# A four-layer transformer pass on one core: TensorE's order written out in the source, attention in bundles, and a wider up-projection

## The chip, the core and the metric

The kernel runs on one NeuronCore of a Trainium2 chip, in one launch. The metric is device time in microseconds (us) of that core; a profile of one execution lies beside the timed runs. TensorE does the matmuls, with its weight loads shown apart (PEld). VectorE (DVE) and ScalarE (ACT) do the elementwise work, GpSimd (POOL) a few powers and some DMA issues, SyncE (SP) issues most DMAs.

## The reference, cut to what matters

Two blocks of two layers each act on x of 256 tokens by 1024 features, in float32. Every layer is attention, a residual, and an MLP with another residual.

```python
# block 1
x = x + concat(diff_attention(q, k, v), memory_attention(qm, mem)) @ a_w_out      # layer a
x = x + relu(rms(x) @ a_w_up) ** 2 @ a_w_down                                     # 1024 -> 4096 -> 1024
x = x + concat(moba_attention(q, k, v), memory_attention(qm, mem)) @ b_w_out      # layer b
x = x + relu(rms(x) @ b_w_up) ** 2 @ b_w_down
x = rms(x) * final_norm
# block 2
h = h + rms(stick_breaking(q, k, v) @ sb_w_o) * g                                 # 16 heads of 64
h = h + rms(conv_ffn(rms(h)))                                                     # 1024 -> 2 x 2816 -> 1024, gated
h = h + rms(forgetting(q, k, v, fcum) @ fox_w_o) * g
h = h + rms(conv_ffn(rms(h)))
```

conv_ffn is `gelu(conv3(gate)) * conv3(up)` followed by the down-projection. Diff attention is softmax minus lambda times a second softmax, with a norm for each head; with 256 tokens the moba layer is plain causal attention with rope.

## The kernel before

**Numbers in halves.** Weights and activations are float32. Each is split into a high half, rounded to float32r (whi, yTh, L169 or L179 on ScalarE), and the rest (wlo, yTl, L170 or L180 on VectorE). A product is three matmuls, high x high, high x low and low x high (mm3, L206 to L210). The split weights live in eight buffers of 128 x 1024 for each half (W_BUFS, tags whi and wlo), the raw weights in three (RAW_BUFS).

**Projections.** mm_rows (L278) makes a tile of 128 tokens by up to 512 columns: for each of eight k two matmuls with the token tile's high half as weights (L282, L283), then eight with its low half (L285). columns_T (L300) makes 128 columns of y @ w transposed, with all 256 tokens as the moving columns: eight times mm3 in 256 columns.

**MLP.** up_pair (L498) makes two chunks of 128 features in one bank with columns_T; the first group goes by up_tokens (L505), a row tile at a time, and is transposed afterwards. The result goes through relu and a square (mlp, L554) or through the convolution, gelu and product (conv_ffn, L569), is split (u_split, L490) and put to Down (L523), which adds the down-projection up in four banks. Down.put issues the matmuls of the item before; the last three items are done a row tile at a time, with finish(t) after each.

**Attention.** quad (L427) does four heads for a query tile: scores (L344, matmuls on L349), a softmax (soft, L392) or the stick-breaking weights (stick, L410), transposes of the weights (blocks_T, L383, L387), attention times v (L436; L900 in the forgetting layer) and out_T (L403). The differential layer has its own diff (L688), with its heads' norm on "on" (L712) and a transpose. The layers (layer_a L663 on, layer_b, layer_sb, layer_fox) call projections and quads in the order of the source.

**What sets the order.** The order on every engine, TensorE's too, is set by a scheduler from the dependencies, a cost model and the order of the source as priority: a later projection can go ahead of a score that isn't ready, and a group of attention matmuls is cut up and strewn among a projection's. issue_after (L198) holds a few splits back by hand. The eight PSUM banks: two "acc", two "sc", two "ht", one "pt", one "po".

## Time and profile before

| | |
|---|---|
| median of 3 runs | 1265.97 us (1265.57 to 1266.2) |
| span of the profiled execution | 1265.0 us |
| TensorE busy | 1245.0 us (98%), 7791 matmuls |
| weight loads | 1083.7 us (86%) |
| VectorE busy | 873.0 us (69%) |
| ScalarE busy | 744.8 us (59%) |
| DMA | 211.77 MB, mean 167 GB/s |

A busy time is the sum of what one engine had in work. Matmuls are pipelined and their ends are modelled: the spacing of their starts tells what one costs in a stream, not its duration. The stages in order of time: memory keys and values and the start of layer a up to about 52 us, layer a's attention to 150, its MLP to 335, layer b's attention to 450, its MLP to 635, stick breaking to 760, the first gated FFN to 950, forgetting attention to 1075, and the second gated FFN.

### The profile page before, as it was taken

To read this page: it belongs to the slowest core of one execution; us is meant where nothing else is said; L and a number is where in the kernel's file an instruction comes from. 1 tells how busy PE (TensorE), PEld (TensorE's weight loads), DVE (VectorE), ACT (ScalarE), POOL (GpSimd) and SP (SyncE) were. 2 spreads that over 40 slices of the span, in tenths; PEclk is the share of its full clock that TensorE was granted. 3 is DMA by queue.
4 is the path that set the end of the run, shared out by engine and by line. 5 is a ranking of instruction groups with operands and counts; after the bars stand their busy time and mean duration, and the time that the engine had idled before them with its cause. 6 is when DMAs were issued, how large, how long until landed. Compare 5 with 4: busy or idle time off the path is not lost.

```text
span 1265.0 us, 20179 instructions
## 1 busy us (share of the span) xinstructions
PE 1245.0 (98%) x7791; PEld 1083.7 (86%) x7791; DVE 873.0 (69%) x1687; ACT 744.8 (59%) x1386; POOL 43.0 (3%) x73
## 2 busy tenths in 40 slices
PE   8999999999999999999999999999999999999997
PEld 6776789999876789999889778999989987999996
DVE  5778755565887665556567888667678876877675
ACT  7656654444766655445556778555567755855552
POOL 1201100000000000000000000000001000000000
PEclk9999999999999999999999999999999999999999
DMA  9643356464454165646373426555537443655550
GB/s 318 215 167 107 113 174 223 153 214 166 155 178 132 40 210 186 215 152 211 132 240 134 134 79 199 194 169 179 198 96 254 139 149 102 214 191 185 170 173 34
DMA packets 129552, 211.77 MB, mean 167 GB/s; under 512 B 5368, under 2 KB 86624, under 8 KB 129456
## 3 DMA queue, kind: packets, MB, share of 16 engines
q1 hardware_dynamic: 127616, 207.25, 49.0%
q0 software_dynamic: 1696, 3.17, 0.8%
q8 instruction: 61, 1.00, 0.3%
q14 instruction: 35, 0.29, 0.1%
q10 hardware_dynamic: 144, 0.07, 0.0%
HBM read 209.36 MB, written 1.10 MB: 166 GB/s over the span
## 4 chain that ended last, share of the span: by engine, by line
PE 92%; ACT 3%; DVE 2%; DMA 1%; issue 1%; POOL 1%; SPq 0%; POOLq 0%; DVEq 0%; ACTq 0%
PE acc L208 12%; PE acc L209 12%; PE acc L210 12%; PE sc L210 10%; PE sc L208 10%; PE sc L209 10%; PE acc L282 5%; PE acc L283 5%; PE acc L285 5%; PE sc L349 4%; PE tp L387 2%; PE tp L436 2%; PE tp L251 1%; ACT junk L231 1%; DVE wlo L170 1%
## 5 line engine op out<-in xcount | busy, mean ns | idle before, releaser
L170 DVE TENSOR_TENSOR wlo<-raw,whi 128x1024 fp32r<-128x1024 f32 x336 | 403.3, 1221 | 167.3 <-ACT whi L169 163.5
L169 ACT ACTIVATE whi<-raw 128x1024 fp32r<-128x1024 f32 x336 | 343.8, 1055 | 169.8 <-PE acc L210 75.3
L210 PE MATMUL sc<-yTh,wlo 128*128 128x256 f32 x1088 | 308.0, 283 | 0.0
L209 PE MATMUL sc<-yTl,whi 128*128 128x256 f32 x1088 | 308.0, 283 | 0.0
L208 PE MATMUL sc<-yTh,whi 128*128 128x256 f32 x1088 | 307.8, 283 | 0.0
L208 PEld LDWEIGHTS sc<-yTh,whi 128*128 128x128 f32 x1088 | 208.6, 192 | 2.3 <-issue 0.5
L209 PEld LDWEIGHTS sc<-yTl,whi 128*128 128x128 f32 x1088 | 208.6, 192 | 1.7
L210 PEld LDWEIGHTS sc<-yTh,wlo 128*128 128x128 f32 x1088 | 208.6, 192 | 0.1
L208 PE MATMUL acc<-whi,u 128*128 128x512 f32 x432 | 169.2, 392 | 0.0
L209 PE MATMUL acc<-wlo,u 128*128 128x512 f32 x432 | 168.8, 391 | 0.0
L210 PE MATMUL acc<-whi,u 128*128 128x512 f32 x432 | 167.0, 390 | 0.0
L282 PE MATMUL acc<-whi,yTh 128*128 128x512 f32 (+3 forms) x336 | 132.3, 397 | 0.4
L283 PE MATMUL acc<-wlo,yTh 128*128 128x512 f32 (+3 forms) x336 | 130.4, 391 | 0.0
L587 DVE SCALAR_TENSOR_TENSOR cv<-sc,conv,cv 128x255 f32<-128x255 f32 (+1 forms) x160 | 76.2, 479 | 36.7 <-ACT cv L585 35.1
L210 PEld LDWEIGHTS acc<-whi,u 128*128 128x128 f32 x432 | 81.1, 188 | 17.4 <-DVE u L495 0.4
L208 PEld LDWEIGHTS acc<-whi,u 128*128 128x128 f32 x432 | 81.3, 188 | 16.4 <-ACT u L494 0.9
L209 PEld LDWEIGHTS acc<-wlo,u 128*128 128x128 f32 x432 | 81.3, 188 | 14.9
L285 PE MATMUL acc<-whi,yTl 128*128 128x512 f32 (+3 forms) x336 | 85.0, 387 | 0.0
L179 ACT ACTIVATE whi<-raw,g_late 128x256 fp32r<-128x256 f32 (+4 forms) x160 | 71.5, 520 | 18.3 <-PE acc L209 11.1
L180 DVE SCALAR_TENSOR_TENSOR wlo<-raw,g_late,whi 128x256 fp32r<-128x256 f32 (+4 forms) x160 | 72.5, 507 | 11.8 <-ACT whi L179 11.7
L282 PEld LDWEIGHTS acc<-whi,yTh 128*128 128x128 f32 x336 | 63.9, 190 | 12.9 <-ACT yTh L261 2.1
L208 PE MATMUL acc<-yTh,whi 128*128 128x256 f32 x256 | 74.3, 290 | 0.0
(193 smaller groups left out, 1751.5 us busy)
## 6 DMA issues: line engine op xcount, KB each, us to landing
raw<-in_w_up SPq DMA_DIRECT2D x88, 512.0 KB, 4.7
raw<-in_w_down SPq DMA_DIRECT2D x22, 1024.0 KB, 5.4
raw<-in_a_w_up SPq DMA_DIRECT2D x16, 1024.0 KB, 5.5
raw<-in_a_w_down SPq DMA_DIRECT2D x16, 1024.0 KB, 4.9
raw<-in_b_w_up SPq DMA_DIRECT2D x16, 1024.0 KB, 5.4
raw<-in_b_w_down SPq DMA_DIRECT2D x16, 1024.0 KB, 4.8
raw<-in_a_w_in SPq DMA_DIRECT2D x16, 512.0 KB, 5.8
raw<-in_sb_w_qkv SPq DMA_DIRECT2D x16, 512.0 KB, 4.5
```

What stands on the lines that cost most here:

```text
L169: act(hv, rv[:, k0:k1], AF.Copy)
L170: V.tensor_tensor(lv, rv[:, k0:k1], hv.bitcast(F32), op=ALU.subtract)
L179: act(hv[:, k - k0, o:e], rv[:, k, o:e], AF.Copy, scale=gk)
L180: V.scalar_tensor_tensor(lv[:, k - k0, o:e], rv[:, k, o:e], gk, hv[:, k - k0, o:e].bitcast(F32), op0=ALU.mult, op1=ALU.subtract)
L208: mm(acc, lhsT=a[0], rhs=b[0], start=start, stop=False)
L209: mm(acc, lhsT=a[0], rhs=b[1], start=False, stop=False)
L210: mm(acc, lhsT=a[1], rhs=b[0], start=False, stop=stop)
L282: mm(acc, lhsT=h, rhs=ws[k][0], start=k == 0, stop=False)
L283: mm(acc, lhsT=h, rhs=ws[k][1], start=False, stop=False)
L285: mm(acc, lhsT=tslice(yT, k, t)[1], rhs=ws[k][0], start=False, stop=k == KC - 1)
L349: mm(sv[:, i], lhsT=q[i][:, t * P:(t + 1) * P], rhs=k[i][:, :nk], start=True, stop=True)
L587: V.scalar_tensor_tensor(hi[:, sh:], pi[:, :S - sh], cw(tap, ch), hi[:, sh:], op0=ALU.mult, op1=ALU.add)
```

## The change

1. **Order.** TensorE's order is that of the source (manual_schedule); the other engines are still scheduled. The layers are rewritten so that projection row tiles (slot), transposed column blocks (col) and parts of the output projection (OutProj.run with a list of chunks) alternate with bundles (between): first the transposes left over from the slot before (flush), then the attention times v (PV) of earlier quads, then transposes (T) and scores (SC) of others. A quad is cut into s, tr and pv, which are called slots apart.
2. **MLP.** columns_2T multiplies the high half of the weights with both halves of y in one matmul of 512 columns (two pieces of 256), and the low half with y's high half in 256. yT is one tile for both halves. ScalarE copies the columns of the low half out of PSUM, VectorE adds the others. relu and square become one VectorE operation.
3. **PSUM.** "sc" becomes two double banks, for scores, for transposes of weights and rows and for the up-projection; "ht" and "po" have one bank each, "pt" is gone. The row tile 1 accumulators of OutProj and Down lie on "ht" and "po".
4. **The ends of stages.** finish and fin return the transposes of their row tile, to be placed by whoever follows: those of tile 0 into the matmuls of tile 1, those of tile 1 (turn) behind the first row tiles of the next stage. out_proj_end places the last bundles between the parts of tile 1's output projection.
5. **Blocks.** Layers a and b project 512 columns of q or of k at once where they had 256 of each; layer_sb and layer_fox keep one block of v for its second row tile until after the last column block.

The diff, cut to its core:

```diff
+    ctx.enter_context(tc.manual_schedule(engines={nc.tensor.engine}))
     def acc_tile(i=0):
-        tag = ("acc", "pt", "po")[i]
+        tag = ("acc", "ht", "po")[i]
-    def sc_tile():
-        return pp.tile([P, 512], F32, name="sc", tag="sc", bufs=2)
+    def sc_tile(name="sc"):
+        return pp.tile([P, 2, 512], F32, name=name, tag="sc", bufs=2)
...
+    def columns_2T(acc, yT, ws, o):
+        a = acc.rearrange("p (h s) -> p h s", h=2)
+        for k in range(KC):
+            h, l = (w[:, o:o + P] for w in ws[k])
+            mm(a, lhsT=h, rhs=yT[2][:, :, k, :], start=k == 0, stop=False)
+            mm(a[:, 0], lhsT=l, rhs=yT[0][:, k, :], start=False, stop=k == KC - 1)
...
+    def slot(b, t, T=(), PV=(), SC=()):
+        f = b.half(t)
+        between(T, PV, SC)
+        if f is not None:
+            later.append(f)
+    def between(T=(), PV=(), SC=()):
+        flush()
+        for q in PV:
+            q.pv()
+        one = len(T) < 2 and len(SC) < 2
+        for f in ([q.s for q in SC] if one else []) + [q.tr for q in T] + ([] if one else [q.s for q in SC]):
+            f()
...
     def up_pair(yT, ws, o):
         s = sc_tile()
         for i in range(2):
-            columns_T(s[:, i * S:(i + 1) * S], yT, ws, o + i * P)
-        return s
+            columns_2T(s[:, i], yT, ws, o + i * P)
+        u = t512("ur")
+        uv = u.rearrange("p (i s) -> p i s", s=S)
+        act(uv, s[:, :, S:], AF.Copy)
+        V.tensor_tensor(uv, s[:, :, :S], uv, op=ALU.add)
+        return u
...
+            if g == 0:                       # mlp
+                first = UpTokens(yT, ws)
+                first.half(0)
+                turn()
+                first.half(1)
+                first.turn(0)
             for j in range(2):
-                r = rs[j]
-                if r is None:
-                    r = t512("r")
-                    act(r, up_pair(yT, ws, j * 256), AF.Relu)
-                u = t512("u")
-                V.tensor_tensor(u, r, r, op=ALU.mult)
-                dn.put(u_split(u), g * 2 + j)
-        dn.end()
+                if g == 0 and j == 0:
+                    continue
+                if g == 0:
+                    first.turn(1)
+                rs = first.pair if g == 0 else [up_pair(yT, ws, j * 256)]
+                for i, r in enumerate(rs):
+                    u = t512("u")
+                    V.scalar_tensor_tensor(u, r, 0.0, r, op0=ALU.max, op1=ALU.mult)
+                    dn.put(u_split(u), g * 2 + (i if g == 0 else j))
+        return dn.end()
...
+        slot(Q0, 1, SC=[d00])                # layer a, from its fourth row tile on
+        slot(KV, 0, T=[d00], SC=[d20])
+        tables()
+        slot(KV, 1, T=[d20], PV=[d00], SC=[d01])
+        d00.turn()
+        slot(VV, 0, T=[d01], SC=[d21])
+        slot(VV, 1, T=[d21], PV=[d20, d01])
+        slot(Q1, 0, PV=[d21])
+        d20.turn()
+        d01.turn()
+        slot(Q1, 1, SC=[d40, m[0]])
+        d21.turn()
+        op.run(0, [0, 1, 2, 3])
+        between(T=[d40, m[0]], SC=[d41, m[1]])
+        m[0].out = "sc"
+        between(PV=[d40, m[0]])
+        op.run(0, [6, 7])
+        d40.turn()
+        between(T=[d41, m[1]])
...
+        V0.load()                            # layer sb
+        V1.load()
+        slot(V0, 0)
+        slot(V1, 0)
+        turn()
+        slot(V0, 1)
         R = along_rows(rs)
+        col(0)
+        col(1)
+        col(2)
+        between(SC=[a0])
+        col(3)
+        between(SC=[b0])
+        col(4)
+        between(T=[a0], SC=[a2])
+        col(5)
+        between(T=[b0], PV=[a0], SC=[b2])
+        col(6)
+        between(T=[a2], PV=[b0], SC=[a4])
+        col(7)
+        between(T=[b2], PV=[a2], SC=[a6])
+        slot(V1, 1, T=[a4], PV=[b2], SC=[b4])
+        op.run(0, [0, 1, 2, 3])
...
+        col(1)                               # layer fox
+        slot(VB, 0, SC=[a0])
+        col(2)
+        between(T=[a0], SC=[b0])
...
+        col(7)
+        between(PV=[a2], SC=[a3])
+        slot(VB, 1, T=[b1], SC=[b3])
+        op.run(0, [0, 1, 2, 3])
+        between(T=[a3, b2], PV=[b1])
+        op.run(0, [4, 5])
+        between(PV=[a3, b2], T=[b3])
```

Block.half(t) is mm_rows of one row tile with its evacuation; heads_block returns the transposes of q or k as what is flushed later; col(i) makes 128 columns of q and of k with columns_T, loading weights for two such columns at every even i.

## Rows read from the trace of the kernel before

**Rows 1.** The page, part 1: busy us, share of span, instructions.

```profile
PE 1245.0 (98%) x7791; PEld 1083.7 (86%) x7791; DVE 873.0 (69%) x1687; ACT 744.8 (59%) x1386; POOL 43.0 (3%) x73
```

**Rows 2.** Windows, us: busy (instructions) of each engine, PEclk, DMA share, GB/s.

```profile
640.00:745.00 105.00, 104.99 (x709) 87.40 (x708) 78.92 (x139) 69.12 (x126) 0.54 (x1) 1.00 0.40 132
680.00:700.00 20.00, 19.99 (x148) 16.76 (x147) 17.68 (x36) 15.68 (x31) 0.00 (x0) 1.00 0.35 127
765.00:945.00 180.00, 179.85 (x1250) 167.68 (x1249) 132.06 (x188) 106.60 (x153) 1.09 (x2) 1.00 0.55 181
950.00:1055.00 105.00, 104.86 (x775) 94.68 (x775) 81.19 (x266) 69.70 (x188) 6.35 (x11) 1.00 0.52 165
```

**Rows 3.** TensorE's timeline, gated FFN: start, us, line, out<-in; first and last of each.

```profile
809.99 0.28 PE L208 MATMUL sc<-yTh,whi 128*128 128x256 f32 x1
...
814.55 0.28 PE L210 MATMUL sc<-yTh,wlo 128*128 128x256 f32 x1
...
815.14 0.39 PE L210 MATMUL acc<-whi,u 128*128 128x512 f32 x1
...
819.91 0.39 PE L210 MATMUL acc<-whi,u 128*128 128x512 f32 x1
```

**Rows 4.** Groups by line (the last: 985 to 1055 us): count | busy, mean ns | idle before.

```profile
L208 PE MATMUL sc<-yTh,whi 128*128 128x256 f32 x1088 | 307.8, 283 | 0.0
...
L170 DVE TENSOR_TENSOR wlo<-raw,whi 128x1024 fp32r<-128x1024 f32 x336 | 403.3, 1221 | 167.3 <-ACT whi L169 163.5
...
L169 ACT ACTIVATE whi<-raw 128x1024 fp32r<-128x1024 f32 x336 | 343.8, 1055 | 169.8 <-PE acc L210 75.3 <-PE sc L209 55.5 <-PE acc L285 19.1
...
L180 DVE SCALAR_TENSOR_TENSOR wlo<-raw,g_late,whi 128x256 fp32r<-128x256 f32 x32 | 14.0, 480 | 3.0 <-ACT whi L179 2.9
```

**Rows 5.** TensorE's timeline, stick breaking: two runs of attention times v (L436).

```profile
689.95 0.28 PE L208 MATMUL acc<-yTh,whi 128*128 128x256 f32 x1
690.20 0.43 PE L436 MATMUL tp<-pT,vt 128*64 128x128 f32 x2
690.56 0.38 PE L209 MATMUL acc<-yTl,whi 128*128 128x256 f32 x1
690.79 0.28 PE L210 MATMUL acc<-yTh,wlo 128*128 128x256 f32 x1
...
692.58 1.09 PE L436 MATMUL tp<-pT,vt 128*64 128x128 f32 x14
```

**Rows 6.** TensorE's timeline: score runs (L349) in stick breaking and the moba layer.

```profile
677.64 0.28 PE L208 MATMUL acc<-yTh,whi 128*128 128x256 f32 x1
677.85 1.13 PE L349 MATMUL sc<-kT,qT 64*128 64x256 f32 x4
678.90 0.39 PE L209 MATMUL acc<-yTl,whi 128*128 128x256 f32 x1
...
383.79 1.62 PE L349 MATMUL sc<-mkTb,qmT 64*128 64x256 f32 x8
```

**Rows 7.** Timelines of ScalarE and VectorE where layer a's MLP begins.

```profile
163.08 0.58 ACT L512 ACTIVATE ut<-acc 128x512 f32<-128x512 f32 x1
...
164.51 0.64 ACT L520 ACTIVATE ur<-tp 128x256 f32<-128x256 f32 x2
...
165.79 1.28 DVE L565 TENSOR_TENSOR u<-ur 128x512 f32<-128x512 f32 x2
...
166.50 1.23 ACT L494 ACTIVATE u<-u 128x512 fp32r<-128x512 f32 x2 [0.41 <-DVE u L565]
```

**Rows 8.** TensorE's timeline, differential layer, and its waits: total us, times, longest.

```profile
130.97 0.60 PE L387 MATMUL tp<-con,e 128*128 128x128 f32 x4
...
133.47 0.33 PE L251 MATMUL tp<-con,on 128*128 128x128 f32 x1 [0.74 <-DVE on L712]
...
PE tp L251 <- DVE on L712: 2.6, 4, 0.7
```

**Rows 9.** Waits in the stick-breaking stage, 640 to 745 us.

```profile
ACT whi L169 <- PE acc L209: 13.8, 3, 7.6
```

More of the change, by code (lines that the diff above doesn't have):

```diff
@@ L461, in run @@
                     self.ws[k2], self.ws[k2 + 1] = rows(self.w, k2)
+        def run(self, t, ks):
+            if t not in self.acc:
+                self.acc[t], self.left[t] = [acc_tile(c + 1 if t else 0) for c in range(2)], KC
+            a, first = self.acc[t], self.left[t] == KC
+            self.left[t] -= len(ks)
+            self.load(ks)
+            last = self.left[t] == 0
+            todo = [(k, c) for c in range(2) for k in ks] if last else [(k, c) for k in ks for c in range(2)]
+            for k, c in todo:
                 b = tuple(h[:, c * 512:(c + 1) * 512] for h in self.ws[k])
-                mm3(a[c], tslice(self.oT, k, t), b, k == self.order[0], k == self.order[-1])
+                mm3(a[c], tslice(self.oT, k, t), b, first and k == ks[0], last and k == ks[-1])
             return a
@@ L542, in go @@
                     todo.sort(key=lambda e: e[4])
-                for u, j, wd, i, c in todo:
+                for n, (u, j, wd, i, c) in enumerate(todo):
+                    if then is not None and n == len(todo) * 3 // 4:
+                        then()
+                        then = None
                     o = i * S + t * P
@@ new lines, in layer_a @@
+        d00, d20, d40, d01, d21, d41 = (dq[h, t] for t in range(NT) for h in (0, 2, 4))
+        slot(K0, 0)
+        slot(K0, 1)
+        slot(Q0, 0)
+        slot(Q0, 1, SC=[d00])
+        slot(KV, 0, T=[d00], SC=[d20])
+        tables()
+        slot(KV, 1, T=[d20], PV=[d00], SC=[d01])
[6 more added lines that the diff above has]
+        slot(Q1, 1, SC=[d40, m[0]])
@@ L789, in layer_sb @@
+    def layer_sb(yT, rs, turn, fin):
         w = d["sb_w_qkv_2"][0]
```

660 lines of the change are left out of this document (365 added, 295 removed).

## The prediction

> **What bounds the kernel now.** I read the page's busy times first, then the windows by stage, then TensorE's timeline in three places. TensorE is busy for 1245.0 of 1265.0 us [rows 1], and its granted clock stands at 1.00 in every stretch of [rows 2]. So only fewer or cheaper matmuls, or fewer gaps between them, shorten the span. A busy engine is not one at its peak, so look at starts, not durations. In the up-projection 38 steps of a 256-column matmul take 809.99 to 814.55, 120 ns each; in the down-projection 21 steps of a 512-column matmul take 815.14 to 819.91, 227 ns each [rows 3]. Twice the columns cost 1.89 times as much, so every matmul carries some 13 ns that doesn't depend on its columns. There are no waits in these stages. The attention stages are where the small matmuls lie: on the timeline they form 57 unbroken runs of score matmuls (L349) and 51 of attention times v (L436, L900), one of each kind in [rows 5, 6]. VectorE is second: 78.9 of 105 us in the stick-breaking stage, with 17.7 of 20 in its middle, and 81.2 of 105 in the forgetting stage [rows 2].
>
> **Wider up-projection (gain).** L208 to L210 issue three 256-column matmuls for each of 1088 pairs of chunk and k [rows 4]. columns_2T issues one of 512 (the high half against both halves of y) and one of 256. By starts: 3 x 120 = 360 ns before, 227 + 120 = 347 after, 12.9 ns less [rows 3]; x 1088 = 14.0 us. All of it is on TensorE, the path that sets the end. The new moving operand is two pieces of 256 columns; no row shows such a matmul. Bounds: 227 ns (the row of one piece) and 240 (two matmuls), that is 14.0 or 0 us. I take 14.0, as the columns are the same.
>
> The Trainium skill, "TensorE: Matmul & The Clock Gate", section "Back-to-back issue gap", says that a warm matmul costs N/2.4 + 2.5 ns. By that rule a matmul saved is worth 2.5 ns and this part 2.7 us. The trace disagrees: 120 and 227 ns where the rule has 109 and 216.
>
> Each pair of chunks now has to be added up: ScalarE copies one half out of PSUM (in the MLP in the place of L563) and VectorE adds the other, about 0.7 us by the nearest row, two L565 in 1.28 [rows 7]. In the gated FFN this brings VectorE from 132 to about 146 us over 20 pairs, in a stage that falls from 180 to about 176 us [rows 2], 83%. The cover is the next pair's 5.6 us of matmuls in the other of two double banks; I cost it at nothing. Without cover it would be up to 1.3 us for each of 68 pairs.
>
> **Attention in bundles (gain).** A run has a price besides its matmuls. PV: a run of two lies between starts at 689.95 and 690.56, 0.49 us more than the ordinary 0.12, and the next gap is 0.23, 0.11 too long: 0.60 in all. Fourteen take 1.09 us where two take 0.43, 0.055 us each, so a run's price is 0.60 - 0.11 = 0.49 us [rows 5]. Scores: four of 256 keys between 677.64 and 678.90 cost 1.14 us over the ordinary gap; four more add 1.62 - 1.13 = 0.49, so a run's price is 0.65 us [rows 6]; for 128 keys I estimate less and take 0.55 on average. Reading the slot and between calls in order, 51 PV runs become 22: 29 x 0.49 = 14.2 us. Of the 44 score runs with 64 rows (the first three layers) 20 are left: 24 x 0.55 = 13.2 us. The forgetting layer's 66-row scores I take at nothing (bounds 0 and 5 x 0.65 us). Sum 27.4 us. The differential layer's transposes of "on", for which TensorE waits 2.6 us in four places [rows 8], are put later: 2.6 us.
>
> **New waits (loss).** TensorE now follows the source, so whatever isn't ready stops all that follows. The trace shows hardly any such waits; I price them from durations, and where I call a value an estimate its bounds are nothing and twice it.
> 1. Start of each MLP. After UpTokens.turn(1), put(u1) emits the Down matmuls of u0 at once. Their operand needs the copy of acc (0.58), the copies of the transposes (0.64 for two), the square (0.64 of 1.28) and the high half (about 0.63) one after the other [rows 7], with handovers some 3.8 us, and the low half 0.8 later; the transposes themselves fill about 0.9 and other work on the two engines adds some. Today up-projection matmuls of the next group lie between. I take 3.2 us, twice: 6.4 (bounds 2 x 2 and 2 x 5).
> 2. One "po" bank for two PVs in a bundle. The differential pair d20, d01 waits for the chain through L712: transposes of "on" come 2.5 us after the PV ends (130.97 to 133.47) [rows 8]. Three bundles of quads wait for out_T, a ScalarE copy and a VectorE subtraction: by the shortest copies and subtractions of [rows 4, 7], 0.3 and 0.5, with handovers 1.1 us, an estimate. 5.8 us.
> 3. Scores that directly follow heads_T of their own q: four places, 0.9 us each for one ScalarE copy and its handovers, an estimate from L520 [rows 7]. 3.6 us.
> 4. OutProj.run on the chunk that was just computed (the memory heads): three places of 0.7, the 1.1 of point 2 less what else is issued there, an estimate. 2.1 us.
> 5. Two softmaxes at once (d40 with m0, a4 with m0, then tile 1) under 24 matmuls, 5.4 us, while ScalarE also splits W_out at 1.05 us a piece (L169) [rows 4]: one such piece in the way, 4 x 1.1 = 4.4 us, an estimate.
> 6. Weight halves in the last two layers. V1 (VB) is loaded early and its second row tile comes after the last column block, so it holds four of the eight whi and wlo buffers; each pair of column blocks must wait for the pair before it to let go. ScalarE already waits for such buffers, 13.8 us in three waits [rows 9], which cost TensorE nothing there. A buffer freed needs one L169 and one L170, 2.4 us together, and the next comes at L170's 1.2 us [rows 4] while TensorE uses one up in 0.72: 2.4 us lost at the first block and 1.9 at the second, little where a bundle lies between. 5 us; and 5 in the forgetting layer, whose split with gains is longer (sixteen L180 for a pair).
> 7. Transposes of row tile 1 directly ahead of its matmuls: 0.6 us.
> Sum 32.9 us, bounds about 16 and 49: each wait half as long, or half as long again. A wait can't be worth less than nothing.
>
> **Moved without price.** Loads keep their order on SP's queue, and the forgetting layer's loads of aug rows on POOL's come one column pair earlier than they are used; DMA engines are busy 0.40 to 0.55 of these stages [rows 2]. Dropping the second gain per tile in the moba layer, and one pT copy for two, takes work off VectorE and ScalarE only.
>
> **Sum.** 1265.0 - 14.0 - 27.4 - 2.6 + 32.9 = 1253.9 us for the profiled span. The median of the three runs is 1.0 us over it, so 1255.
>
> **Rivals.**
> A, the forecast: 1245 to 1263.4.
> B, the bundles pay in full: ScalarE and VectorE run ahead of TensorE as they do today and the waits are half as long: 1255 - 16.5 = 1238.5. For it: today TensorE hardly waits anywhere, and most bundles have a whole row tile of 5.4 us ahead of them. Against: today the order was chosen by what is ready, and now it isn't.
> C, slower: VectorE becomes the bound of the last two layers, because the held buffers keep it from working ahead. Shortened by bundles, the stick-breaking stage would have VectorE at 78.9 of about 96 us as a mean, and what can't be done early falls into its middle, where it stands at 88% now [rows 2]. If half of each column pair's split is exposed (half of four L170, 4.9 us, for each of four pairs in one layer; half of sixteen L180, 7.7 us, for three in the other [rows 4]), 21 us are lost there in place of 10; with waits 1 to 5 a third over my values, another 7: 1273. It decides from 13 us more than my sum of waits.
> D, the 512-column matmul doesn't do what it says: two pieces stream as two matmuls and the 14.0 us fall away: 1269; the equal number of columns in [rows 3] speaks against it. By the Trainium skill's rule above 2.7 us would be left, 1266; the 13 ns of [rows 3] speak against that.
>
> **Chances.** A 0.42, B 0.27, D 0.04, C 0.17, and 0.10 that waits and gains cancel to within 0.2% (2.5 us, about what a measurement of this kernel can tell from no change). Faster 0.69, same 0.14, slower 0.17. A's own range is 1245 to 1263; the range for 8 in 10 takes in most of B and the lower side of C: 1234 to 1272.
>
> **What would show it.** Right: starts of the up-projection 227 and 120 ns apart; some 28 score and 22 PV runs; a TensorE gap of about 3 us ahead of the first Down matmuls of each MLP; gaps at the first column blocks with the release from L170. B would show the same runs with few gaps over 1 us. C would show VectorE over 90% busy in the middle of the last two layers with TensorE waiting for wlo. My number is wrong if the waits of points 2 to 6 are hidden (then too high), or if the copy and the add in the up-projection come late (then too low).

## The result, and the profile after

The changed kernel takes 1381.74 us (median of 4 runs, 1380.39 to 1382.77) where the kernel before takes 1266.09: a ratio of 1.091, 95% interval 1.090 to 1.093. It is 9% slower, and 110 us over the top of the predicted range. No rival of the prediction had this size.

| | before | after |
|---|---|---|
| span of the profiled execution | 1265.0 us | 1380.7 us |
| TensorE busy | 1245.0 us, 7791 matmuls | 1256.3 us, 6703 matmuls |
| span less TensorE busy ("idle" below) | 20.0 us | 124.4 us |
| mean granted TensorE clock | 0.999 | 0.964 |
| VectorE, ScalarE busy | 873.0, 744.8 us | 907.0, 759.3 us |

The page of the kernel after, part 1 (busy us, share of the span, instructions), answers to [rows 1]:

```profile
PE 1256.3 (91%) x6703; PEld 1050.4 (76%) x6703; DVE 907.0 (66%) x1691; ACT 759.3 (55%) x1360; POOL 41.9 (3%) x73
```

TensorE has 1088 matmuls fewer and is still busy 11 us longer, and it stands idle for 104 us more: 104.4 + 11.3 is the 115.7 us by which the spans differ. VectorE is at 66%, ScalarE at 55%: neither has become the bound as an engine. Windows of the kernel after show where it happens (from:to, length, then busy us and instructions of PE, PEld, DVE, ACT, POOL, then PEclk, DMA share, GB/s); they answer to [rows 2]:

```profile
50.00:100.00 50.00, 40.63 (x185) 32.31 (x184) 31.84 (x82) 20.62 (x46) 0.55 (x1) 0.90 0.40 137
...
200.00:250.00 50.00, 42.16 (x183) 34.05 (x183) 23.19 (x30) 21.55 (x34) 0.00 (x0) 0.86 0.36 126
250.00:400.00 150.00, 148.37 (x743) 125.21 (x742) 93.06 (x113) 70.27 (x94) 1.55 (x2) 1.00 0.55 187
...
500.00:550.00 50.00, 37.62 (x175) 29.91 (x174) 25.34 (x40) 23.07 (x42) 1.40 (x1) 0.86 0.36 126
550.00:700.00 150.00, 150.00 (x755) 126.38 (x755) 88.51 (x94) 67.88 (x80) 0.00 (x0) 1.00 0.54 188
```

The inner parts of the MLPs (250 to 400, 550 to 700) run as dense as before, at clock 1.00. The loss lies in the attention stages and where they meet the MLPs. In the three such windows shown TensorE is at 75 to 84%, the granted clock at 0.86 to 0.90, and VectorE and ScalarE at 41 to 64%: no engine is full, so each spends time waiting. The list of waits of TensorE in the kernel after (engine, tile and line <- what ended the wait: total us, times, longest):

```profile
PE tp L279 <- DVE yT L270: 34.6, 8, 6.0
PE tp L279 <- DVE yT L264: 9.4, 6, 1.8
PE acc L212 <- ACT u L559: 8.6, 4, 3.4
PE tp L493 <- DVE yT L450: 7.1, 3, 4.3
PE acc L214 <- DVE yT L450: 6.7, 4, 3.2
PE tp L832 <- DVE on L839: 5.8, 1, 5.8
PE acc L214 <- DVE wlo L174: 4.8, 10, 0.8
...
PE tp L386 <- ACT qT L387: 3.9, 4, 1.4
PE acc L214 <- DVE wlo L184: 3.6, 8, 1.0
PE acc L212 <- ACT yT L449: 3.6, 4, 2.0
...
PE tp L256 <- DVE on L839: 2.7, 1, 2.7
```

The first two lines, 44 us in 14 places, are one piece of code, row_T, which makes a row tile's eight transposes and their copies. It is called 14 times, and each call waits once, between its first four transposes and its second four: 18.8 us in the six calls for row tile 1 of x, 22.0 in the six for row tile 0, 3.2 in the two for the memory rows. In the kernel after it is (comments added)

```python
def row_T(dst, t, xt, g=None):
    tp = sc_tile("tp").rearrange("p c (n k) -> p (c n) k", k=P)   # one tile, two banks
    for c in range(2):
        for i in range(4):
            k = 4 * c + i
            nc.tensor.transpose(tp[:, k, :], xt[:, k * P:(k + 1) * P], ident)   # L279
        last = halves_T(dst, t, tp[:, 4 * c:4 * c + 4], 4 * c, 4, g)   # copies: L263, L264, or with gains L269, L270
    return last
```

With gains halves_T copies a chunk (128 columns) at a time: ScalarE writes its high half (L269), then VectorE subtracts it from the chunk in PSUM, which gives the low half (L270).

The timelines of TensorE, ScalarE and VectorE at one such place of the kernel after (start, us, engine, line, operation, out<-in, count, idle before):

```profile
49.78 0.60 PE L279 MATMUL tp<-con,x 128*128 128x128 f32 x4
56.42 1.12 PE L279 MATMUL tp<-con,x 128*128 128x128 f32 x4 [6.03 <-DVE yT L270]
...
54.15 0.37 ACT L269 ACTIVATE yT<-tp,g_early 128x128 fp32r<-128x128 f32 x1 [0.26 <-DVE yT L270]
55.61 0.37 ACT L269 ACTIVATE yT<-tp,g_early 128x128 fp32r<-128x128 f32 x1 [1.09 <-DVE yT L270]
...
58.36 0.37 ACT L269 ACTIVATE yT<-tp,g_early 128x128 fp32r<-128x128 f32 x1 [0.42 <-DVE yT L270]
59.15 0.37 ACT L269 ACTIVATE yT<-tp,g_early 128x128 fp32r<-128x128 f32 x1 [0.42 <-DVE yT L270]
...
53.77 0.35 DVE L270 SCALAR_TENSOR_TENSOR yT<-tp,g_early,yT 128x128 fp32r<-128x128 f32 x1
...
54.09 1.22 DVE L174 TENSOR_TENSOR wlo<-raw,whi 128x1024 fp32r<-128x1024 f32 x1
55.23 0.35 DVE L270 SCALAR_TENSOR_TENSOR yT<-tp,g_early,yT 128x128 fp32r<-128x128 f32 x1
56.01 0.35 DVE L270 SCALAR_TENSOR_TENSOR yT<-tp,g_early,yT 128x128 fp32r<-128x128 f32 x1 [0.43 <-ACT yT L269]
```

Three things lie on top of one another here. TensorE has written the first four chunks, and the next four go into the same tile (its other bank), so it waits until VectorE has read the last of the first four: 6.03 us with nothing to do, because in the fixed order nothing may pass. ScalarE starts a chunk only when VectorE is done with the chunk before (54.15 after 53.77 + 0.35; 55.61 after 55.23 + 0.35), so the copies of a tile are one chain; with nothing between its links the step is 0.79 us a chunk (58.36 to 59.15), 3.2 us for four. And VectorE puts a split of weights (L174, 1.22 us) between two links of that chain. In the kernel before the two halves lie on two tiles, with a chain each. Its timelines where the last row tile of the forgetting stage is copied:

```profile
1074.62 1.59 ACT L261 ACTIVATE yTh<-tp,g_late 128x128 fp32r<-128x128 f32 x4 [2.17 <-PE tp L251]
...
1075.02 1.57 DVE L262 SCALAR_TENSOR_TENSOR yTl<-tp,g_late,yTh 128x128 fp32r<-128x128 f32 x4 [0.76 <-ACT yTh L261]
```

Four chunks go through both engines in 1.97 us there (1074.62 to 1076.59), 0.4 a chunk; which chunk lies on which tile the trace doesn't name. The waits of ScalarE for VectorE at these copies, summed over the run, are 4.0 us in 14 places before and 24.5 us in 51 places after.

The clock is the second part of the loss. TensorE's timeline at the start of layer a's MLP in the kernel after:

```profile
218.80 0.80 PE L212 MATMUL acc<-whi,u 128*128 128x512 f32 x1 [3.36 <-ACT u L559]
...
221.92 0.63 PE L214 MATMUL acc<-whi,u 128*128 128x512 f32 x1
222.35 0.63 PE L212 MATMUL acc<-whi,u 128*128 128x512 f32 x1
222.77 0.63 PE L213 MATMUL acc<-wlo,u 128*128 128x512 f32 x1
...
225.09 0.39 PE L214 MATMUL acc<-whi,u 128*128 128x512 f32 x1
225.32 0.39 PE L212 MATMUL acc<-whi,u 128*128 128x512 f32 x1
```

After an idle stretch of 3.36 us the 512-column matmuls start 0.425 us apart; from 224.41 on they start 0.227 us apart, as in [rows 3]. The granted clock of 218.8 to 222.9 is 0.50 in the windows (1.2 GHz of 2.4). So such a wait is paid for again in the slow matmuls after it. Over the whole profile the granted clock is 0.50 for 98.3 us, and TensorE is busy in 83.1 us of them. By the two spacings 47% of that busy time would go at full clock: an estimate of 38.7 us.

### The profile page after: what moved, and what is told of

Its sections match the earlier page's. It is cut to its first block, busy times and chain, and to the rows that moved or that the text cites. A ratio compares the mean times of both kernels' runs of the same rounds, so it can differ in the third digit from the quotient of the medians.

```text
span 1380.7 us, 17828 instructions
## 1 busy us (share of the span) xinstructions
PE 1256.3 (91%) x6703; PEld 1050.4 (76%) x6703; DVE 907.0 (66%) x1691; ACT 759.3 (55%) x1360; POOL 41.9 (3%) x73
## 4 chain that ended last, share of the span: by engine, by line
PE 75%; DVE 12%; ACT 8%; issue 3%; POOL 0%; DMA 0%; SPq 0%; DVEq 0%; POOLq 0%; ACTq 0%
PE sc L305 18%; PE acc L214 10%; PE acc L212 10%; PE acc L213 9%; PE sc L306 9%; PE acc L290 5%; PE acc L291 5%; DVE wlo L174 4%; PE acc L293 3%; ACT whi L173 2%; PE tp L433 1%; DVE wlo L184 1%; PE sc L395 1%; ACT whi L183 1%; PE tp L279 1%
## 5 line engine op out<-in xcount | busy, mean ns | idle before, releaser
L174 DVE TENSOR_TENSOR wlo<-raw,whi 128x1024 fp32r<-128x1024 f32 x336 | 403.4, 1220 | 142.7 <-ACT whi L173 139.5
L173 ACT ACTIVATE whi<-raw 128x1024 fp32r<-128x1024 f32 x336 | 343.3, 1053 | 170.2 <-PE acc L214 69.0
L305 PE MATMUL sc<-yT,whi 128*128 128x512 f32 x1088 | 386.1, 398 | 0.0
L306 PE MATMUL sc<-yT,wlo 128*128 128x256 f32 x1088 | 305.4, 281 | 0.0
L305 PEld LDWEIGHTS sc<-yT,whi 128*128 128x128 f32 x1088 | 204.4, 188 | 50.6
L306 PEld LDWEIGHTS sc<-yT,wlo 128*128 128x128 f32 x1088 | 205.5, 189 | 1.6
L214 PE MATMUL acc<-whi,u 128*128 128x512 f32 x432 | 171.2, 396 | 1.4 <-DVE u L560 1.4
L290 PE MATMUL acc<-whi,yT 128*128 128x512 f32 (+3 forms) x336 | 142.7, 426 | 3.0 <-ACT whi L183 2.8
L291 PE MATMUL acc<-wlo,yT 128*128 128x512 f32 (+3 forms) x336 | 138.3, 412 | 0.0
L212 PEld LDWEIGHTS acc<-whi,u 128*128 128x128 f32 x432 | 82.6, 191 | 27.9 <-ACT u L559 10.3
L214 PEld LDWEIGHTS acc<-whi,u 128*128 128x128 f32 x432 | 82.5, 191 | 21.9 <-DVE u L560 3.8
L676 DVE SCALAR_TENSOR_TENSOR cv<-ur,conv,cv 128x254 f32<-128x254 f32 (+1 forms) x176 | 76.9, 479 | 12.9 <-ACT cv L674 11.4
L290 PEld LDWEIGHTS acc<-whi,yT 128*128 128x128 f32 x336 | 70.8, 211 | 19.0 <-ACT whi L183 2.9
L214 PE MATMUL acc<-yT,wlo 128*128 128x256 f32 x256 | 76.1, 297 | 8.5 <-DVE wlo L174 4.8
L291 PEld LDWEIGHTS acc<-wlo,yT 128*128 128x128 f32 x336 | 70.1, 209 | 13.3 <-DVE wlo L184 0.7
L293 PE MATMUL acc<-whi,yT 128*128 128x512 f32 (+3 forms) x336 | 79.9, 380 | 0.0
```

The source lines that it names most:

```text
L173: act(hv, rv[:, k0:k1], AF.Copy)
L174: V.tensor_tensor(lv, rv[:, k0:k1], hv.bitcast(F32), op=ALU.subtract)
L212: mm(acc, lhsT=a[0], rhs=b[0], start=start, stop=False)
L214: mm(acc, lhsT=a[1], rhs=b[0], start=False, stop=stop)
L290: mm(acc, lhsT=h, rhs=ws[k][0], start=k == 0, stop=False)
L291: mm(acc, lhsT=h, rhs=ws[k][1], start=False, stop=False)
```

## Experiments

Each line gives the median, the ratio to the kernel before with its 95% interval, and from one profile TensorE's busy time, idle time (span less busy) and mean granted clock. "Busy" holds more than work: a matmul at half clock, or one that stands between its issue and its end, counts as busy. e7 to e10 have two runs each; those of e9 lie 4.9 us apart, those of e7 2.4.

| kernel | us | ratio | busy | idle | clock |
|---|---|---|---|---|---|
| before | 1266.1 | 1 | 1245.0 | 20.0 | 0.999 |
| after | 1381.7 | 1.091 (1.090 to 1.093) | 1256.3 | 124.4 | 0.964 |
| e1 row tiles | 1351.5 | 1.068 (1.066 to 1.069) | 1254.7 | 95.1 | 0.975 |
| e2 MLP start | 1367.5 | 1.081 (1.079 to 1.082) | 1248.5 | 115.1 | 0.969 |
| e3 before, with the wide up-projection | 1269.8 | 1.003 (1.002 to 1.004) | 1241.0 | 26.7 | 0.997 |
| e4 after, scheduled | 1262.5 | 0.997 (0.996 to 0.998) | 1221.5 | 41.2 | 0.996 |
| e5 e4 and row tiles | 1259.1 | 0.994 (0.993 to 0.996) | 1219.7 | 37.5 | 0.997 |
| e6 e5 with the narrow matmuls | 1265.0 | 0.999 (0.998 to 1.000) | 1225.9 | 36.8 | 0.996 |
| e7 e1 and e2 | 1339.3 | 1.058 (1.056 to 1.060) | 1251.0 | 85.3 | 0.977 |
| e8 no low split | 1345.0 | 1.062 (1.060 to 1.064) | 1244.5 | 99.4 | 0.971 |
| e9 e7 on two tiles | 1320.3 | 1.043 (1.040 to 1.045) | 1235.0 | 81.1 | 0.983 |
| e10 e9 and PV banks | 1306.5 | 1.032 (1.030 to 1.034) | 1234.9 | 70.2 | 0.985 |
| e11 e5 on two tiles | 1256.3 | 0.992 (0.991 to 0.993) | 1219.5 | 35.0 | 0.997 |
| e12 e10 and early row tiles | 1297.5 | 1.024 (1.022 to 1.025) | 1233.2 | 64.0 | 0.981 |
| e13 e11 with one piece | 1257.4 | 0.992 (0.991 to 0.993) | 1219.7 | 36.0 | 0.997 |
| e14 e13 and PV banks | 1253.3 | 0.989 (0.988 to 0.991) | 1217.4 | 33.7 | 0.997 |

### Is it the fixed order? (e4)

```diff
-    ctx.enter_context(tc.manual_schedule(engines={nc.tensor.engine}))
```

> The changed kernel without manual_schedule: the source stays, but TensorE's order is the scheduler's again. Theory F (the source's order is what turns a late operand into a stop): TensorE goes on with other matmuls at the shared tile and at the start of the MLPs, the half-clock stretches go, and the time comes below 1290 us. Rival V (VectorE and ScalarE bound, whatever TensorE's order): above 1340 us.

Measured 1262.45 us: with all else kept, giving TensorE's order back to the scheduler returns 119 us. The page of e4, part 1:

```profile
PE 1221.5 (97%) x6703; PEld 1018.5 (81%) x6703; DVE 901.1 (71%) x1691; ACT 753.9 (60%) x1360; POOL 41.8 (3%) x73
```

The same 6703 matmuls are busy 1221.5 us where they were busy 1256.3 in the fixed order, 34.8 us less, at a clock of 0.996 against 0.964; idle falls by 83. In e4 the granted clock is 0.50 for 8.9 us, with TensorE busy in 6.5 of them. By the estimate above that is 3.0 us of lost busy time where the kernel after has 38.7: the difference, 35.7, is the size of the 34.8 measured. No run changes the clock alone. The rest of the change is worth 3.7 us over the kernel before (ratio 0.997), and this version leaves 21 us more idle than it.

### The row tiles (e1, and e5 in the scheduled order)

```diff
-        for c in range(2):
-            for i in range(4):
-                k = 4 * c + i
-                nc.tensor.transpose(tp[:, k, :], xt[:, k * P:(k + 1) * P], ident)
-            last = halves_T(dst, t, tp[:, 4 * c:4 * c + 4], 4 * c, 4, g)
+        for k in range(8):
+            nc.tensor.transpose(tp[:, k, :], xt[:, k * P:(k + 1) * P], ident)
+        for c in range(2):
+            last = halves_T(dst, t, tp[:, 4 * c:4 * c + 4], 4 * c, 4, g)
```

> The changed kernel with one edit: row_T issues all eight transposes first and the evacuations of both halves after them. Theory S (shared tile): in the changed kernel the second four transposes write into the tile whose first four ScalarE and VectorE are still reading, so TensorE, bound to the source's order, stands still for 44 us in 13 places, and TensorE's clock halves after some of them. Then this edit takes away the 44 us and with them part of the half-clock stretches: 1300 to 1335 us, TensorE waiting on yT at the transposes for under 5 us in all, mean granted clock above 0.975. Rival V (VectorE and ScalarE are the bound and TensorE waits for them anyhow): the waits turn up again at the matmuls that read yT, and the time stays above 1360 us.

Measured 1351.48 us, 30 less: between the two expectations. The 44 us of waits at the transposes are gone, and a part has moved to the matmuls that read the row tile next. TensorE's waits in e1 at that place:

```profile
PE acc L289 <- ACT yT L269: 10.6, 15, 1.3
```

So issuing all eight transposes before the first copy removes the wait for the tile, but not the chain of copies: of theory S the cause holds, not its range, for some 30 of 44 us come back. What is left is the chain (e9).

> The changed kernel with TensorE's order left to the scheduler (as in e4_scheduled) and row_T's eight transposes ahead of its evacuations (as in e1_rows). If the order is what turned the shared tile into a stop, the edit is worth little here, as the scheduler puts other matmuls between: 1258 to 1263 us, against 1262.5 of e4_scheduled. If the tile itself costs, 1245 us or less.

Measured 1259.1 us, 3.4 less than e4 and inside the first range: where TensorE may go on with other matmuls, the same edit is worth a ninth.

### The chain of copies (e8, e9, e11)

Two causes stood for the length of the chain: VectorE's queue, which holds splits ahead of the copies, and the alternation of the two engines on one PSUM tile. e8 takes VectorE's splits away and leaves out the weights' low halves (cut):

```diff
+    zlo = cst.tile([P, 1024], F32R, name="zlo")
+    V.tensor_copy(zlo, z0)
...
-            lo = wp.tile([P, 1024], F32R, name="wlo", tag="wlo", bufs=W_BUFS)
...
-            lv = lo[:, :(k1 - k0) * n].rearrange("p (k n) -> p k n", n=n)
+            lv = zlo[:, :(k1 - k0) * n].rearrange("p (k n) -> p k n", n=n)
...
-                V.tensor_tensor(lv, rv[:, k0:k1], hv.bitcast(F32), op=ALU.subtract)
...
-                        V.scalar_tensor_tensor(lv[:, k - k0, o:e], rv[:, k, o:e], gk,
-                                               hv[:, k - k0, o:e].bitcast(F32), op0=ALU.mult, op1=ALU.subtract)
```

> The changed kernel without VectorE's splits of the weights: the low halves of all weights are one constant tile of zeros, so the results leave out high activation times low weight, while every matmul is still issued. It takes about 470 us of work from VectorE and the wait for free wlo buffers. Theory Q (TensorE's stops are long because the evacuation it waits for stands in VectorE's queue behind weight splits of 1.2 us each): the waits at the transposes fall from 44 us to under 25, all gaps from 131 to under 85, and the time to 1300 to 1330 us. Rival L (it is the bare chain of ScalarE and VectorE, with nothing ahead of it): above 1360 us.

Measured 1344.95 us, 37 less, with VectorE's busy time halved (468.6 us). Neither theory got its numbers. The waits at the transposes in e8:

```profile
PE tp L280 <- DVE yT L271: 30.6, 8, 5.0
PE tp L280 <- DVE yT L265: 8.9, 6, 1.8
```

They fell only from 44.0 to 39.5 us with VectorE's splits away. So VectorE's queue makes little of them; the splits' cost is spread over other places (idle fell by 25 us, up to 8.4 of them because nobody waits for wlo any more). ScalarE's own splits (L173) stayed, and their share was not tested apart. That left the alternation. e9, against e7:

```diff
-        tp = sc_tile("tp").rearrange("p c (n k) -> p (c n) k", k=P)
+        tps = [sc_tile("tp")[:, 0].rearrange("p (n k) -> p n k", k=P) for c in range(2)]
         for k in range(8):
-            nc.tensor.transpose(tp[:, k, :], xt[:, k * P:(k + 1) * P], ident)
+            nc.tensor.transpose(tps[k // 4][:, k % 4, :], xt[:, k * P:(k + 1) * P], ident)
         for c in range(2):
-            last = halves_T(dst, t, tp[:, 4 * c:4 * c + 4], 4 * c, 4, g)
+            last = halves_T(dst, t, tps[c], 4 * c, 4, g)
```

> The kernel with both edits (row tiles and MLP start), and in row_T the eight transposes lie on two PSUM tiles of four chunks, one bank each, in the place of one tile of eight. Theory K: the copies of a row tile's transposes are one chain, because ScalarE may read chunk i+1 of a PSUM tile only when VectorE is done with chunk i of it (0.39 us a step, 16 steps, 6.3 us on one tile); on two tiles the two chains run beside each other, about 3.5 us. Then the 23.8 us for which ScalarE waited for VectorE at these copies fall below 8, TensorE's waits at the row tiles' matmuls (19.8 us of gaps there) fall to 8 to 13, and with the clock's share the time is 1322 to 1332. Rival Q: the copies are late because VectorE's queue holds splits of weights ahead of them; then two tiles change nothing much: 1336 to 1343.

Measured 1320.32 us, 19 less than e7, somewhat more than expected (its two runs are 1317.9 and 1322.8). The waits of ScalarE in e7, then in e9, and the timelines of e9 at one row tile:

```profile
ACT yT L269 <- DVE yT L270: 23.8, 45, 1.7
...
ACT yT L269 <- DVE yT L270: 5.8, 10, 1.4
...
177.50 3.11 ACT L269 ACTIVATE yT<-tp,g_late 128x128 fp32r<-128x128 f32 x8
...
177.89 3.10 DVE L270 SCALAR_TENSOR_TENSOR yT<-tp,g_late,yT 128x128 fp32r<-128x128 f32 x8 [1.98 <-ACT yT L269]
```

Eight chunks go through both engines in 3.49 us (177.50 to 180.99), where one tile needs 0.79 us a chunk, 6.3 in all. The wait of ScalarE for VectorE falls from 23.8 us in e7 to 5.8. The chain on one tile is shown as the main cause of what e1 left. Little of the gain is idle time: between the profiles of e7 and e9 idle falls by 4.2 us and busy by 16.0. Half of the 16.0 is the clock by the estimate above (50.6 us busy at clock 0.50 in e7, 33.9 in e9: 7.8). The rest fits matmuls that follow the copies: at one row tile of e7 eight pairs of L289 and L290 start 0.79 us apart (188.39 to 193.89), the pace of the chain; in e9 the first four do (177.91 to 180.27), and then 0.46.

The Trainium skill, "PSUM — Partial Sum Buffer", section "PSUM bank collisions raise a hardware error", says that two engines must not touch one bank and partition quadrant at the same time, two readers included, and that the compiler back end's scheduler adds a dependency between such instructions. The lock step of L269 and L270 within one bank agrees with that. But here it goes by the tile and not by the bank: a tile of e7 lies on two banks, four chunks in each, and its eight chunks still come 0.79 us apart (188 to 194 us), over the border of the banks too; e9 has four chunks in each of two banks as well, and only the tiles are two.

> The scheduled order with the row tile edit, and row_T's transposes on two PSUM tiles. Theory K: of 5.7 us that TensorE still waits for these copies about half go, and what ScalarE and VectorE get done earlier is worth a little more: 1254 to 1258. Rival: both double banks taken at once hold up the scores and the up-projection that use them, 1259 to 1264.

Measured 1256.33 us, 2.8 less than e5: theory K, again small where the order is free.

### The start of the MLP (e2, e7)

```diff
+                us = []
-                for i, r in enumerate(rs):
+                for r in rs:
                     ...
-                    dn.put(u_split(u), g * 2 + (i if g == 0 else j))
+                    us.append(u_split(u))
+                if g == 0:
+                    dn.pend += [(us[0], 0), (us[1], 1)]
+                else:
+                    dn.put(us[0], g * 2 + j)
+        while len(dn.pend) > dn.keep + 1:
+            dn.go([dn.pend.pop(0)])
```

> The changed kernel with one edit: in the first group of each MLP the Down matmuls of u0 are put behind the next up-projection pair, where the changed kernel has them directly behind the transposes of the first group. Theory M (the prediction's first wait): the two waits of 3.6 us ahead of the first Down matmuls go, and the half-clock stretches behind them: 1368 to 1376 us. Rival: TensorE would wait there anyhow for the next group's weight halves: 1380 us or more.

Measured 1367.5 us, 14.2 less: theory M. Both waits of 3.4 us are gone, and with them two of together 1.4 us for the low half of u just behind (L214 <- DVE u L560): 8.1 us of waits, worth 14.2. In the profiles idle fell by 9.3 us and busy by 7.8. The busy time at clock 0.50 fell from 83.1 to 67.4, by the estimate above 7.3 us; of that some 5.1 lie in the slow matmuls behind the two waits (218.8 to 224.4, and 539.2 to 545.3), and the rest in stretches elsewhere, which differ between the two profiles.

> The changed kernel with both repairs, row_T's transposes first and the Down matmuls of u0 behind the next up-projection pair. If the two waits are independent, their gains add: 1382 - 30 - 14 = 1338 us (1333 to 1343), and what is left over the kernel before, some 70 us, lies in other waits of the fixed order. If one only moved what the other had hidden, 1345 us or more.

Measured 1339.34 us: the gains of e1 (30.3) and e2 (14.2) add up to 44.5, and 42.4 came.

### The bank of attention times v (e10, e14)

```diff
+        d01.out = ("sc", "ht")
...
+        b0.out = m[0].out = "sc"
...
+        b2.out = "sc"
```

> As the run with two tiles, and the second attention times v of each bundle (d01, b0 and m0 in the moba layer, b2 in the forgetting layer) lies on its own bank, taken from the double banks. Theory: the wait of a second one for the only po bank costs 12 to 14 us of gaps (5.8 for the differential pair, 4.5, 2.1 and 1.2 for the quads), and with the clock's share 13 to 18 us: 9 to 18 us under the run with two tiles. Rival: what is waited for is the next step of the chain (the transposes of on, the output projection), and the waits move there: less than 5 us under it.

Measured 1306.54 us, 13.8 under e9: the theory. The waits of 5.8 and 7.1 us for "po" in the list of the kernel after are gone from e10's; 2.6 us of the rival's kind came back, as the waits of the output projection for out_T grew from 10.2 to 12.8. What the waits for "po" were for is seen in the timelines of the kernel after, in the moba layer's bundle of a4 and m0:

```profile
478.81 0.66 PE L493 MATMUL tp<-pT,vt 128*64 128x128 f32 x8
483.73 1.12 PE L493 MATMUL tp<-pT,mvb 128*64 128x128 f32 x8 [4.26 <-DVE yT L450]
...
481.42 0.45 ACT L424 ACTIVATE e<-sc,nn 128x256 f32<-128x256 f32 x1
481.77 0.19 ACT L424 ACTIVATION_READ_ACCUMULATOR e<-sc,nn 128x1 f32 x1
481.87 0.36 ACT L449 ACTIVATE yT<-tp 128x256 fp32r<-128x256 f32 x1
...
482.67 0.61 DVE L442 TENSOR_SCALAR e<-e,rs 128x256 f32<-128x256 f32 x2
...
483.26 0.42 DVE L450 TENSOR_TENSOR yT<-tp,yT 128x256 fp32r<-128x256 f32 x1
```

out_T itself is 0.36 and 0.42 us; its copy (L449) stands behind the exponentials of two softmaxes (L424) until 481.87, its subtraction (L450) behind their scaling (L442) until 483.26.

### Held weight buffers (e12)

```diff
         slot(V0, 1)
+        slot(V1, 1)
...
-        slot(V1, 1, T=[a4], PV=[b2], SC=[b4])
+        between(T=[a4], PV=[b2], SC=[b4])
...
-        slot(VB, 0, SC=[a0])
+        slot(VB, 0)
+        slot(VB, 1, SC=[a0])
...
-        slot(VB, 1, T=[b1], SC=[b3])
+        between(T=[b1], SC=[b3])
```

> As the run with two tiles and banks of their own for the second attention times v, and in the last two layers the second row tile of V1 and of VB comes before the column blocks, so that its four weight buffers of each half are free for them; its old place keeps the bundle alone. Theory H (held buffers): the column blocks' 8.1 us of waits for wlo (4.8 in the stick-breaking layer, 3.3 in the forgetting layer) fall below 3, and with the clock's share the time falls by 5 to 12 us, to 1295 to 1302. Rival V: the waits for wlo are VectorE's pace, not the buffers, and stay at 6 to 9 us: 1302 to 1308. Rival M: the row tile was the cover of the softmax between two bundles; without it the transposes of the weights (blocks_T) wait 2 to 6 us in each of the two layers, in the place of what the buffers give back: 1303 to 1316.

Measured 1297.46 us, 9.1 under e10: theory H. No wait for wlo is left in the column blocks. Rival M's wait, of blocks_T for the softmax, comes to 0.3 us. Another new wait is there, of a score for k's column block, 3.5 us where e10 has 0.3:

```profile
PE sc L394 <- DVE kT L967: 3.5, 1, 3.5
```

### The wider up-projection (e3, e6, e13)

e3 puts columns_2T, the one yT tile, and the copy and the add of each chunk into the kernel before, and nothing else.

> The kernel before with the wide up-projection alone: high weights against both halves of y in one matmul of 512 columns, each chunk in its own bank, ScalarE's copy and VectorE's add for each chunk; the order on TensorE stays the scheduler's. The prediction's term: 12.9 ns for each of 1088 triples, starts 227 and 120 ns apart, 1252 us (1249 to 1256). Rival P (two pieces stream as two matmuls): starts 240 ns apart, 1266 us. Rival Q (the copy and the add come late and the up-projection waits for its bank): starts right, but 1262 us or more.

Measured 1269.76 us, 3.6 more than the kernel before, and by none of the three expectations: the starts are neither 227 nor 240 ns apart, and the new wait is not for the up-projection's bank. TensorE's timeline in e3 and its first line of waits:

```profile
809.92 0.40 PE L309 MATMUL sc<-yT,whi 128*128 128x512 f32 x1
...
814.87 0.40 PE L309 MATMUL sc<-yT,whi 128*128 128x512 f32 x1
815.10 0.28 PE L310 MATMUL sc<-yT,wlo 128*128 128x256 f32 x1
815.22 0.40 PE L208 MATMUL acc<-whi,u 128*128 128x512 f32 x1
...
PE acc L208 <- ACT u L501: 6.8, 2, 3.4
```

Fifteen pairs take 809.92 to 815.22, 353 ns each (235 and 118), where three narrow matmuls take 360 [rows 3] and I had 347. So a pair saves 6.7 ns (353.3 against 360), 7.3 us for 1088. Against it stand two waits of 3.4 us at the starts of the gated FFNs, for the operand of the first Down matmuls, which comes later by the copy and the add: the cover that I had counted on isn't there for the first item. TensorE's busy time falls by 4.0 us and idle grows by 6.7. The clock takes most of the rest of the 7.3: behind the two waits it is at 0.50, with TensorE busy for 6.5 us, by the estimate above 3.0 us lost.

e6 takes the wide matmul alone out of e5 (the copy by ScalarE stays, VectorE's add goes):

```diff
-            columns_2T(s[:, i], yT, ws, o + i * P)
+            columns_T(s[:, i, :S], yT, ws, o + i * P)
-        act(uv, s[:, :, S:], AF.Copy)
-        V.tensor_tensor(uv, s[:, :, :S], uv, op=ALU.add)
+        act(uv, s[:, :, :S], AF.Copy)
```

> e5_sched_rows with the up-projection in three matmuls of 256 columns again; the copy by ScalarE stays, the add by VectorE goes. The wide matmuls took 235 and 118 ns by their starts where 227 and 120 were expected, 353 against 360 for three narrow ones: by that the wide form is worth 7.3 us and this kernel is 7 us slower than e5_sched_rows (bounds 5 and 9). If the copy and the add cost more than that, as the kernel before with the wide form alone suggests (3.6 us slower), this kernel is the faster one.

Measured 1264.96 us, 5.9 more than e5, and busy 6.2 more: the wide matmul is worth 6 us, net of VectorE's adds (41 us of its busy time), which go with it.

e13 asks whether its two pieces are to blame for the 235 ns:

```diff
-        y = ap_.tile([P, 2, KC, S], F32R, name="yT", tag="yT", bufs=2)
-        return y[:, 0], y[:, 1], y
+        y = ap_.tile([P, KC, 2, S], F32R, name="yT", tag="yT", bufs=2)
+        return y[:, :, 0], y[:, :, 1], y
...
-            mm(a, lhsT=h, rhs=yT[2][:, :, k, :], start=k == 0, stop=False)
+            mm(a, lhsT=h, rhs=yT[2][:, k], start=k == 0, stop=False)
```

> The scheduled order with row_T on two PSUM tiles, and yT laid out as k, half, token in the place of half, k, token: the 512 columns of the up-projection's moving operand are one piece of memory in the place of two of 256. Theory P (pieces): the two pieces are what makes the matmul 235 ns in the place of 227; starts come 227 and 118 to 120 ns apart, 1088 x 8 ns = 8.7 us less: 1246 to 1250. Rival A: the 8 ns belong to the 512 columns followed by a 256-column matmul with other weights, whatever the layout: the spacing stays at 235 and the time at 1254 to 1258. Rival E: ScalarE and VectorE write the halves with a larger step, or one buffer's reads and writes meet, and the time is over 1258.

Measured 1257.44 us, no less than e11 (1256.33). TensorE's timeline in e13:

```profile
803.79 0.40 PE L303 MATMUL sc<-yT,whi 128*128 128x512 f32 x1
804.02 0.28 PE L304 MATMUL sc<-yT,wlo 128*128 128x256 f32 x1
...
806.97 0.40 PE L303 MATMUL sc<-yT,whi 128*128 128x512 f32 x1
```

Nine pairs in 3.18 us, 353 ns each, as before: rival A. One piece or two is the same; what makes the pair longer than 227 + 120 stays open.

> As the run with one piece, and the second attention times v of a bundle on a bank of its own, as in the fixed order, where that was worth 13.8 us. Theory F (the wait for the po bank costs only where TensorE may not go on with something else): within 2 us of the run with one piece. Rival: it is worth 4 us or more in the scheduled order too.

Measured 1253.32 us, 4.1 less than e13: the rival, at its edge. In the scheduled order the banks are worth a third of what they were in the fixed one, not nothing. Which wait they take away there is not shown: e13's list has none of the attention times v for "po". e14 is the fastest version, 1.1% under the kernel before (ratio 0.989, 0.988 to 0.991).

## Why the prediction was wrong, step by step

**The step that failed: new wait 7, "transposes of row tile 1 directly ahead of its matmuls: 0.6 us", and no wait at all for row tile 0.** The mechanism was named: TensorE follows the source, so whatever isn't ready stops all that follows. Its price here was not. The 0.6 us is the length of four transposes (0.60 in [rows 8]); the copies that the next four must wait for have no price. Row tile 1 of x cost 18.8 us of waits in six places. Row tile 0, whose transposes the change puts among the matmuls of tile 1, cost 22.0 and stands in no point; the memory rows add 3.2. Of these 44.0 us e1 returned 30.3, and e9 another 19.0 by the chain of copies; the clock's share is in both. What would have shown the price was there: the change section says that transposes of rows move to the double bank "sc", and the timelines of L261 and L262 in the kernel before, where the halves lie on two tiles, show 0.4 us a chunk.

**The second: the granted clock.** I read 1.00 everywhere in [rows 2] and priced matmuls at it, in a kernel whose new waits I had just listed. By the forecast TensorE would be busy for 1203.6 us (1245.0 - 14.0 - 27.4); it was busy for 1256.3, 52.7 more. Of these the half clock is some 38.7 by the estimate above, and e4 bears that out: 34.8 us less busy with 6.5 us at clock 0.50 in the place of 83.1. Some 7 more are the wider up-projection's. The other 74.1 us of the miss are idle time (124.4 where the forecast left 50.3): 43.4 at the row tiles, 10.7 in points 1 to 6 below, and some 20 in waits that no point has, "on" among them.

**The wider up-projection, -14.0.** Mis-sized: 5.9 (e6) to 7.3 us (353 against 360 ns), inside the bounds of 0 and 14.0. The step that failed is the 227 ns for its 512 columns: 235 were measured, one piece or two (e13). The Trainium skill, "TensorE: Matmul & The Clock Gate", section "Back-to-back issue gap", has N/2.4 + 2.5 ns for a warm matmul, by which a matmul saved is worth an estimated 2.5 ns; 5.4 (5.9 us over 1088) to 6.7 ns were measured. "I cost it at nothing" failed too: 3.4 us at each FFN's start in e3.

**Bundles, -27.4.** The counts came as forecast: on the timeline of the kernel after there are 28 unbroken runs of score matmuls and 22 of attention times v. Their price fits the scheduled order, as far as busy time can say: e6 has the 7791 matmuls of before, 26 score runs of 64 rows where before had 44, and 28 runs of attention times v for 51, and is busy 19.1 us less; by the prediction's prices 18 x 0.55 + 23 x 0.49 = 21.2 (66-row runs, 16 for 13, at nothing). No run takes the bundles alone, so the price is not shown apart from the other edits. And idle time takes much of it back: e6 idles 16.8 us more than before, e14 13.7 with 27.6 less busy.

**"on" transposes, -2.6.** Failed: one wait of 2.7 us for "on" is left in the kernel after, and a second stands in the wait for "po" (5.8).

**New waits 1 to 6, +32.9 with 7.** Point 1: 3.4 us at each of two starts where 3.2 stood, right as a wait, but worth 14.2 us to remove with what stood behind it. Point 2: 12.9 us of waits (5.8 and 7.1) where 5.8 stood, and 13.8 in time. I had priced out_T alone, 1.1 us; it stood in line behind the softmaxes that the bundle had just issued, 4.3 us in the longest case (the timelines under e10). Point 3: scores after heads_T waited 0.8, its own second half of transposes for the single "ht" bank 3.9 (L386), 4.7 where 3.6 stood, at another place. Point 4: the output projection waits 10.3 us for out_T (6.7 and 3.6) where 2.1 stood, undersized: 4.4 in layers a and b, which the point meant, and 5.9 in the stick-breaking layer, which it didn't name. Point 5: no wait for the softmaxes' own results of this size shows; they cost as what stands ahead of out_T in point 2. Point 6: 8.4 us (4.8 and 3.6) where 10 stood, and e12 returned 9.1: right in cause and size. Together points 1 to 6 come to 43.0 us of waits where 32.3 stood, inside the bounds of 16 and 49; with points 4 and 5 as far off as they are, that is luck in part.

**The rivals.** C had the sign but not the mechanism: it put the loss into the last two layers, by VectorE as the bound. But some 90 of the 115.7 us were lost before the stick-breaking layer begins (at about 725 us where it was 635), with VectorE at half in the windows above; e8 halves VectorE's work and leaves 1345. The range failed because its bounds, every wait half as long or half as long again, were put around a list without row tile 0, with 0.6 us for row tile 1, and at full clock.

**The balance.** From after to e12 the repairs are 30.3 (row tiles), 14.2 less 2.1 (MLP), 19.0 (two tiles), 13.8 (PV banks), 9.1 (buffers): 84.3 us, 1381.7 to 1297.5. The scheduled order stands at 1253.3 with most of the same edits. The 44 us between them are 46 in the profiles, 30 of idle time and 16 of busy time. The 16 are the clock by the estimate above (TensorE is busy at 0.50 for 39.7 us in e12 and 3.4 in e14: 16.9 us). The 30 are spread over many small waits (the largest line of e12's list is 4.9 us in four places); which of them would go by another order was not tried.

## What to carry to other kernels

When an order that was chosen by readiness is replaced by one that is written out, look first for every place where TensorE writes to a PSUM tile twice or reads something one or two engines have just been asked for, and price the whole chain with its handovers and with the queue that the other engine has at that time, not the operation alone. Copies out of PSUM that two engines make by turns on one tile are a serial chain; give each chain its own tile, and issue all that TensorE has for the tile ahead of the first copy. And price the clock too: waits removed here were worth between about once (e10, e12) and 1.8 times (e2, 14.2 us for 8.1) their length.

## What was not expected of the hardware

- Around idle stretches of TensorE the granted clock fell to 0.50, and matmuls after them ran slow: 512-column ones 0.425 us apart in the place of 0.227 (218.8 to 224.4 in the kernel after). Over the run the mean granted clock was 0.964 at 124 us of idle time, 0.969 to 0.985 between 64 and 115 us, and 0.996 to 0.999 between 20 and 41 us.
- A 512-column matmul followed by a 256-column one with other weights takes 235 and 118 ns (e3), against 227 and 120 in streams of one size [rows 3]; the sum is the same 353 ns whether its columns are one piece of memory or two (e13).
